# Seven products in the first feed-forward stage as in the other two; state-space parameters divided over the first two of these stages

## The chip, the cores and the metric

The kernel runs on one core of a Trainium2 chip. The core has five engines with a queue of instructions each: TensorE (PE in the profile; its weight loads are PEld), VectorE (DVE), ScalarE (ACT), GpSimd (POOL) and SyncE (SP, which issues the DMAs). Each queue is executed in order, and engines wait for each other by semaphores. The metric is device time of one execution in microseconds.

## The reference

A stack of three blocks on x of 512 positions by 1024 features, all in float32. The first two blocks (`hybrid_layer`, layers 0 and 1) mix by attention, a convolution and retention, and then feed forward with 4096 hidden features. The third (`second_block`) mixes by differential attention and a state-space layer and then feeds forward with a gated stage of 2816. Cut to what the change touches:

```
def hybrid_layer(x, ...):
    ...                                        # mixing, x = x + rms_norm(mix)
    h = rms_norm(x, g_mlp_pre)
    f = jnp.square(jax.nn.relu(h @ w_up)) @ w_down
    return x + rms_norm(f, g_mlp_post)

def s5_layer(u, a_re, a_im, log_dt, b_re, b_im, c_re, c_im, ...):
    dt = jnp.exp(log_dt)[:, None]
    mag = jnp.exp(a_re * dt)
    lb_re, lb_im = mag * jnp.cos(a_im * dt), mag * jnp.sin(a_im * dt)
    ...                                        # cr, ci; bb = (cr, ci) * b
    _, _, xr, xi = lax.associative_scan(...)   # a complex linear recurrence over positions
```

What the state-space layer needs of `dt`, `lb` and `b`, `c` depends on the weights alone, so it can be computed at any time before the third block.

## The kernel before

**Precision.** A float32 matmul is made of three passes over operands split into a high part (fp32r) and the rest: high by high, high by low, low by high (`mm3`). Every weight chunk (128x1024, 512 KB) is loaded into `wraw`, its high part is written by ScalarE or VectorE into `whi`, and the rest by VectorE or GpSimd into `wlo`. Which of the two is set by `wbias`: 3 leans to GpSimd, 1 keeps it on VectorE.

**A feed-forward stage.** The normalised input stands transposed in `hhi`/`hlo` (8 blocks of 128 features by 512 positions). A block of 128 hidden features is made (up), passed through square-ReLU into `fhi`/`flo`, and each group of four blocks is multiplied by its part of `w_down` into eight accumulators `acc` (down). The first four blocks are made in two halves of the positions (`f_split`), which overlaps with the end of the normalisation.

Two forms of up exist. In the plain form (`mlp_plain`, layer 0) a block is 8 x 3 matmuls of 512 columns. In the form with seven products (`mlp`, layer 1, and `ffn2` in the third block) two blocks are made together: weights and input are halved along features and positions, and seven products of sums of halves (4 x 3 matmuls of 256 columns each) give the four quarters that eight products gave. The sums and splits of the input are made once (`fast_in`, tiles `sraw`, `shi`, `slo`), those of the weights for each pair (`take_fast`, tiles `wsum`), and the quarters are put together while they leave the accumulators (`FastUp.out`, tiles `mid` and `cu`), all on VectorE and ScalarE. Four of the 32 blocks stay plain, so there are 14 pairs. In this form X is written to DRAM at the start of the stage (`spill`) and read back at its end. `FAST` (line 48) lists the layers that use it; it also sets the order of the weight stream.

**The parameters of the state-space layer** are a side task, a generator that adds its instructions in portions. `ssm_params` (line 1802) first computes on tiles of 128x32 (`prm`) on VectorE with three functions on ScalarE, then eight combinations of 128x512 on GpSimd (`sbc` is the input, results go to DRAM as `gd` and `hd`), then powers of a rotation (`pw`), then eight tables of sines and cosines: two memsets on VectorE, 42 doubling steps on GpSimd (tiles `t`), and at the end one multiply by a sign on VectorE,

```
V.tensor_scalar(Sn, Sn, sgn, None, op0=ALU.mult)
```

which must wait for GpSimd. `yield 3000` says that the next portion is due 3 us later.

**The order of the work** is made ahead of time by a planner (`Trace.order`). It goes through a planned run with a cost for each operation: of the operations whose inputs are ready, an engine takes the one that is due first, and only those due within 25.16 us of the matmul stream's position. The queues of the engines are fixed by it. What the plan takes for shorter or longer than it is shows on the chip as a wait in a queue.

Of the kernel before, what the change touches and what calls it, by code (L numbers as in the profile page):

```python
# [44 lines left out]


NF2 = DFF2 // 128
FAST = (1,)


def mlp_groups():
# [116 lines left out]
PV = {}  # L168
# [768 lines left out]
class Builder:  # L937
# [711 lines left out]
    def mlp_plain(self, l, X):  # L1649
        nc = self.nc  # L1650
        groups = mlp_groups()
        self.wbias = 3
        if l == 0:
            self.side.add(self.ssm_params(), 40000)
        acc = [None] * NT
        f = {}
        last_g = len(groups) - 1

        def relu2(m):
            def ev(ps):  # L1660
                r = self.s2()
                nc.vector.tensor_scalar(r, ps, 0.0, None, op0=ALU.max)
                hi, lo = self.s2(F32R, "fhi"), self.s2(F32R, "flo")
                nc.scalar.activation(hi, r, AF.Square)
                nc.scalar.activation(r, r, AF.Square)
                nc.vector.tensor_tensor(lo, r, hi.bitcast(F32), op=ALU.subtract)
                f[m] = (hi, lo)
            return ev
        lhs = lambda k, t0, t1: tuple(z[:, t0:t1] for z in f[k])
        for g, (k0, n) in enumerate(groups):  # L1670
            if g == 0:
                self.f_split([relu2(i) for i in range(n)], self.mid_start((1, 3)))
                gpost = self.load_gain(4 * l + 3)
                nxt = 4 * (l + 1) if l + 1 < LAYERS else 8
                gpre = self.load_gain(nxt)
            else:
                for i in range(n):
                    self.f_unit(relu2(k0 + i))
                self.down(groups[g - 1], lhs, acc, f, g == 1)
        xd = [[self.dp.tile(F32, f"xd{l}_{t}_{h}", [P, 512]) for h in range(2)] for t in range(NT)]  # L1680

        def store(t):
            for h in range(2):
                nc.sync.dma_start(out=xd[t][h], in_=X[t][h])
        self.finish_plain(groups[-1], lhs, acc, X, gpost, gpre, store)
        self.xd = xd
# [21 lines left out]
    def mlp(self, l, X):  # L1708
        nc = self.nc
        self.wbias = 1  # L1710
        self.seven = True
        xm = self.spill(X, f"xm{l}")
        del X
        f, acc = {}, [None] * NT
# [87 lines left out]
    def ssm_params(self):  # L1802
# [34 lines left out]
        mag = new()  # L1837
        nc.scalar.activation(mag, x, AF.Exp)
        ang = mul(aim, dt)
        yield 3000  # L1840
        k = x
        V.tensor_scalar(k, ang, 1.0 / (2 * math.pi), 12582912.0, op0=ALU.mult, op1=ALU.add)
        V.tensor_scalar(k, k, -12582912.0, None, op0=ALU.add)
# [5 lines left out]
            V.scalar_tensor_tensor(r, k, -c, r, op0=ALU.mult, op1=ALU.add)  # L1849
        V.tensor_scalar(r, r, -3.1415925, 3.1415925, op0=ALU.max, op1=ALU.min)  # L1850
        si, co = new(), new()
        yield 3000
        nc.scalar.activation(si, r, AF.Sin)
        V.scalar_tensor_tensor(co, r, -1.0, r, op0=ALU.mult, op1=ALU.max)
        V.tensor_scalar(co, co, -1.0, math.pi / 2, op0=ALU.mult, op1=ALU.add)
        nc.scalar.activation(co, co, AF.Sin)
        yield 3000
        lb = (mul(mag, co), mul(mag, si))
        nr = new()
        V.tensor_scalar(nr, lb[0], -1.0, None, op0=ALU.add)  # L1860
# [2 lines left out]
        mul(aim, aim, s1)  # L1863
        add(den, s1, den)
        V.reciprocal(den, den)
        yield 3000
        cr, ci = new(), new()
        mul(nr, are, s1)
        mul(lb[1], aim, s2_)
# [3 lines left out]
        mul(nr, aim, s2_)  # L1873
        sub(s1, s2_, s1)
        mul(s1, den, ci)
        yield 3000
        ms = k
        mul(mag, mag, ms)
        self.mag4 = mul(ms, ms)
# [26 lines left out]
        for t in range(4):  # L1906
            V.tensor_scalar(q, d[1], nsg[:, 0:1], None, op0=ALU.mult)
            combine(d[0], q, sb[0], sb[1], self.gd[3 - t])
            yield 3000
            if t < 3:  # L1910
                d = cmul(d, lb, d)
                yield 3000
        ee = (d[0], d[1])
        V.tensor_copy(ee[0], lb[0])
        V.tensor_copy(ee[1], lb[1])
# [1 line left out]
        for t in range(4):  # L1917
            V.tensor_scalar(q, ee[0], sgn, None, op0=ALU.mult)
            V.tensor_scalar(q2, ee[1], -1.0, None, op0=ALU.mult)
            combine(q, q2, sb[2], sb[3], self.hd[t])  # L1920
            yield 3000
            if t < 3:
                ee = cmul(ee, lb, ee)
                yield 3000
        del sb
        ph = cmul((co, si), (co, si))
        ph = cmul(ph, ph, ph)
# [1 line left out]
        for j in range(7):  # L1929
            if j:  # L1930
                ph = cmul(ph, ph)
            pw.append(ph)
            yield 3000
        self.ctd = [self.dp.tile(F32, f"ctd{i}", [P, 512]) for i in range(8)]
        self.std = [self.dp.tile(F32, f"std{i}", [P, 512]) for i in range(8)]
        for b in range(8):
# [4 lines left out]
            for j in range(7):  # L1941
# [9 lines left out]
                G.tensor_tensor(t_, c0, pi, op=ALU.mult)  # L1951
                G.tensor_tensor(s1_, s1_, t_, op=ALU.add)
                if j > 3:
                    yield 3000
            V.tensor_scalar(Sn, Sn, sgn, None, op0=ALU.mult)
            nc.sync.dma_start(out=self.ctd[b], in_=C)
            nc.sync.dma_start(out=self.std[b], in_=Sn)
            yield 3000


    def ssm_task(self, us, ud, yd):
# [394 lines left out]
```

## Time and profile before

| | us |
|---|---|
| time, median of 3 runs | 2094.49 (2093.89 to 2096.01) |
| the profiled execution, its own time | 2094.96 |
| its span, first to last instruction | 2093.2 |

| stretch of the span | us |
|---|---|
| first feed-forward stage, from its first evacuation to its first output normalisation | 282.8 to 618.5 |
| second feed-forward stage, the same | 900.5 to 1213.3 |
| third feed-forward stage | about 1750 to the end |

Line 674 is the helper that issues every operation, so the profile's groups are told apart by tiles, not by lines. A row of the timeline has start, duration, engine, operation, written tile and read tiles, and in brackets how long the engine stood before it and for whom.

### The profile page before, as it was taken

The page shows a single profiled execution, that of the slowest core. Times are in us where ns is not written, and L with a number is a line of the kernel's source. Part 1 is how long each engine was busy: PE and PEld are TensorE (multiplying, and loading weights), DVE is VectorE, ACT ScalarE, POOL GpSimd, SP SyncE. Part 2 cuts the span into 40 slices and gives each one's busy share as a digit, 9 for nine tenths or more (in the row PEclk, how much of TensorE's full clock was granted, in tenths as well). Part 3 has the DMA queues.
Part 4 walks back from the last instruction along what each step waited for, and adds up shares of the span by engine and source line. Part 5 has one row for each costly group of instructions (what it writes and reads, how often), then busy time and mean ns, then how long its engine had stood idle before and what let it go on. Part 6 is the DMA issues. An engine that isn't in the chain of part 4 may idle for free. (4 is left out here: it accounts for less than half of the span.)

```text
span 2093.2 us, 30000 instructions
## 1 busy us (share of the span) xinstructions
PE 2009.5 (96%) x11188; PEld 1741.6 (83%) x11188; DVE 1523.1 (73%) x2487; ACT 1041.7 (50%) x1773; POOL 689.2 (33%) x844
## 2 busy tenths in 40 slices
PE   7999999999999999999999999889999999999999
PEld 7988788877888987799988987678777889989998
DVE  5999578534457999576776773688589649889887
ACT  3378443222334387454443445367577336545543
POOL 4662325993104663100000037753663430000000
PEclk9999999999999999999999999999999999999999
DMA  5423234333232422223422564231325422333322
GB/s 191 134 61 121 89 116 133 126 107 111 86 121 91 134 89 103 101 81 94 128 90 92 181 208 118 83 92 55 116 66 169 158 81 61 101 101 101 121 81 91
DMA packets 87874, 229.53 MB, mean 110 GB/s; under 512 B 10673, under 2 KB 20657, under 8 KB 87729
## 3 DMA queue, kind: packets, MB, share of 16 engines
q1 hardware_dynamic: 87728, 227.62, 34.1%
q8 instruction: 88, 1.44, 0.3%
q14 instruction: 58, 0.47, 0.1%
HBM read 206.35 MB, written 21.23 MB: 109 GB/s over the span
## 5 line engine op out<-in xcount | busy, mean ns | idle before, releaser
L674 ACT CAST whi<-wraw 128x1024 fp32r<-128x1024 f32 (+1 forms) x324 | 331.6, 1030 | 439.2 <-PE ps L674 360.2
L674 POOL TENSOR_TENSOR wlo<-wraw,whi 128x1024 fp32r<-128x1024 f32 (+1 forms) x142 | 333.3, 2354 | 488.5 <-ACT whi L674 399.8
L674 PE MATMUL ps<-hhi,whi 128*128 128x256 f32 (+1 forms) x1488 | 453.5, 330 | 8.6 <-DVE acc L674 2.9
L674 PE MATMUL ps<-hlo,whi 128*128 128x256 f32 (+1 forms) x1488 | 451.4, 328 | 10.3 <-DVE hlo L674 10.3
L674 PE MATMUL ps<-hhi,wlo 128*128 128x256 f32 (+1 forms) x1488 | 449.7, 328 | 1.2 <-DVE wlo L674 1.2
L674 PEld LDWEIGHTS ps<-hlo,whi 128*128 128x128 f32 x1488 | 272.3, 193 | 34.7 <-DVE hlo L674 11.5
L674 PEld LDWEIGHTS ps<-hhi,whi 128*128 128x128 f32 x1488 | 272.3, 193 | 34.1 <-issue 3.3
L674 PEld LDWEIGHTS ps<-hhi,wlo 128*128 128x128 f32 x1488 | 271.4, 193 | 24.2 <-DVE wlo L674 1.4
L674 DVE TENSOR_TENSOR wlo<-wraw,whi 128x1024 fp32r<-128x1024 f32 x192 | 237.4, 1242 | 64.9 <-ACT whi L674 64.9
L674 PE MATMUL ps<-whi,fhi 128*128 128x512 f32 x688 | 251.3, 393 | 5.0 <-DVE acc L674 4.2
L674 PE MATMUL ps<-wlo,fhi 128*128 128x512 f32 x688 | 251.8, 392 | 1.6 <-DVE wlo L674 1.6
L674 PE MATMUL ps<-whi,flo 128*128 128x512 f32 x688 | 252.5, 392 | 0.0
L674 DVE TENSOR_TENSOR acc<-ps,acc 128x512 f32<-128x512 f32 x112 | 75.9, 686 | 116.5 <-PE ps L674 116.4
L674 PE MATMUL ps<-whi,hhi 128*128 128x384 f32 (+1 forms) x448 | 153.5, 367 | 5.2 <-DVE vlo L674 3.5
L674 PE MATMUL ps<-wlo,hhi 128*128 128x384 f32 (+1 forms) x448 | 153.9, 367 | 1.2 <-POOL wlo L674 1.2
L674 PEld LDWEIGHTS ps<-whi,fhi 128*128 128x128 f32 x688 | 129.4, 189 | 29.0 <-DVE acc L674 4.6
L674 PE MATMUL ps<-whi,hlo 128*128 128x384 f32 (+1 forms) x448 | 152.7, 367 | 0.0
L674 PEld LDWEIGHTS ps<-wlo,fhi 128*128 128x128 f32 x688 | 129.7, 189 | 26.7 <-DVE wlo L674 2.9
L674 PEld LDWEIGHTS ps<-whi,flo 128*128 128x128 f32 x688 | 129.7, 189 | 24.4
L674 PE MATMUL ps<-shi,whi 128*128 128x256 f32 (+1 forms) x440 | 124.3, 292 | 0.6 <-ACT mid L674 0.6
L674 PE MATMUL ps<-slo,whi 128*128 128x256 f32 (+1 forms) x440 | 124.2, 291 | 0.0
L674 PE MATMUL ps<-shi,wlo 128*128 128x256 f32 (+1 forms) x440 | 124.0, 290 | 0.0
(272 smaller groups left out, 3887.5 us busy)
## 6 DMA issues: line engine op xcount, KB each, us to landing
wraw<-in_wst SPq DMA_DIRECT2D x302, 512.0 KB, 3.7
wraw<-in_wst SPq DMA_DIRECT2D x32, 384.0 KB, 3.1
gain<-in_gains SPq DMA_DIRECT2D x20, 256.0 KB, 4.9
X<-in_x SPq DMA_DIRECT2D x16, 256.0 KB, 5.4
xd<-X SPq DMA_DIRECT2D x16, 256.0 KB, 2.4
X<-xd SPq DMA_DIRECT2D x16, 256.0 KB, 5.7
gated<-t SPq DMA_DIRECT2D x16, 256.0 KB, 2.2
gate<-gated SPq DMA_DIRECT2D x16, 256.0 KB, 4.2
```

Of the source, the lines that this page charges most:

```text
L674: getattr(getattr(self.nc, e), m)(*[r(x) for x in op.args], **{k: r(v) for k, v in op.kw.items()})
```

## The change

Layer 0 joins the form with seven products, so `mlp_plain` is no longer called, and its weights are split on VectorE alone (`wbias` 1 in place of 3). `ssm_params` is cut in two: what comes before the tables is added at the start of the first feed-forward stage, the tables (`ssm_tables`) at the start of the second. Both begin 30 us of planned time after the stage (40 before), and their portions are due every 7 and 8 us instead of every 3.

```
-FAST = (1,)
+FAST = (0, 1)
...
     def mlp_plain(self, l, X):
...
-        if l == 0:
-            self.side.add(self.ssm_params(), 40000)
...
     def mlp(self, l, X):
         nc = self.nc
         self.wbias = 1
         self.seven = True
+        self.side.add((self.ssm_params, self.ssm_tables)[l](), 30000)
         xm = self.spill(X, f"xm{l}")
...
     def ssm_params(self):
...
-        yield 3000
+        yield 7000
...
             pw.append(ph)
-            yield 3000
+            yield 7000
+        self.pw = pw
+
+    def ssm_tables(self):
+        nc, V, pw = self.nc, self.nc.vector, self.pw
+        o, w = PV["sgn"]
+        sgn = self.pvt[:, o:o + w]
         self.ctd = [self.dp.tile(F32, f"ctd{i}", [P, 512]) for i in range(8)]
         self.std = [self.dp.tile(F32, f"std{i}", [P, 512]) for i in range(8)]
         for b in range(8):
...
                 if j > 3:
-                    yield 3000
+                    yield 8000
             V.tensor_scalar(Sn, Sn, sgn, None, op0=ALU.mult)
             nc.sync.dma_start(out=self.ctd[b], in_=C)
             nc.sync.dma_start(out=self.std[b], in_=Sn)
-            yield 3000
+            yield 8000
```

All other `yield 3000` of `ssm_params` become `yield 7000`.

TensorE in the first feed-forward stage, up, before: blocks of 512 columns, here of two accumulators in turn.

```order
L674 MATMUL ps_3521<-hhi_355,whi_3327 128x512
L674 MATMUL ps_3455<-hhi_355,wlo_3300 128x512
L674 MATMUL ps_3521<-hlo_356,whi_3327 128x512
L674 MATMUL ps_3455<-hhi_355,whi_3285 128x512
L674 MATMUL ps_3521<-hhi_355,wlo_3344 128x512
L674 MATMUL ps_3455<-hlo_356,whi_3285 128x512
```

At the same place now: part of one of the seven products, with the sums `shi`/`slo` as its input.

```order
L674 MATMUL ps_3423<-shi_3484,whi_3413 128x256
L674 MATMUL ps_3423<-slo_3512,whi_3413 128x256
L674 MATMUL ps_3423<-shi_3484,wlo_3438 128x256
L674 MATMUL ps_3423<-shi_3495,whi_3413 128x256
L674 MATMUL ps_3423<-slo_3521,whi_3413 128x256
L674 MATMUL ps_3423<-shi_3495,wlo_3438 128x256
```

What moved: the same up products of 28 blocks are now 1176 matmuls of 256 columns instead of 672 of 512. Outside the first stage TensorE's order is the same but for three places of some ten instructions in the second.

VectorE in the first stage, beginning of the parameters, before: `t<-ps` are evacuations of up, `prm16` is the operand that GpSimd's combination reads, the rest of `prm` leads to it.

```order
L674 TENSOR_SCALAR t_3494<-sbc_3447,pv_412 128x512
L674 TENSOR_TENSOR prm1_3394<-prm13_3460,prm9_3413 128x32
L674 TENSOR_SCALAR t_3501<-ps_3392 128x512
L674 TENSOR_TENSOR wlo_3507<-wraw_3319,whi_3491 128x1024
L674 TENSOR_TENSOR prm13_3460<-prm2_3489,prm1_3394 128x32
L674 COPY prm12_3429<-prm0_3380 128x32
L674 TENSOR_SCALAR prm16_3469<-prm13_3460,prm15_3416 128x32
L674 TENSOR_TENSOR flo_3528<-t_3501,fhi_3509 128x512
L674 TENSOR_SCALAR t_3549<-ps_3455 128x512
```

The same portion now, the end of a run of 19 such instructions; `cu<-ps,mid` is an evacuation of a product.

```order
L674 TENSOR_TENSOR prm2_3736<-prm12_3728,prm10_3685 128x32
L674 TENSOR_TENSOR prm0_3632<-prm0_3632,prm1_3688 128x32
L674 TENSOR_TENSOR prm13_3742<-prm0_3632,prm3_3074 128x32
L674 TENSOR_SCALAR prm16_3745<-prm13_3742,prm15_3640 128x32
L674 TENSOR_TENSOR prm0_3632<-prm12_3728,prm9_3711 128x32
L674 TENSOR_TENSOR prm1_3688<-prm13_3742,prm10_3685 128x32
L674 TENSOR_TENSOR prm0_3632<-prm0_3632,prm1_3688 128x32
L674 TENSOR_TENSOR prm1_3688<-prm13_3742,prm9_3711 128x32
L674 COPY prm12_3728<-prm0_3632 128x32
L674 TENSOR_TENSOR prm13_3742<-prm2_3736,prm1_3688 128x32
L674 TENSOR_SCALAR prm16_3745<-prm13_3742,prm15_3640 128x32
L674 TENSOR_TENSOR cu_3822<-ps_3770,mid_3762 128x256
```

What moved: before, evacuations and splits stood between the parameters' instructions; now the first two writes of `prm16` come with nothing between them but such instructions, ahead of an evacuation.

VectorE at the tables, before, in the first stage: memsets of one table (`t_4853`, `t_4855`), then the sign multiply of the table before it (`t_4659`).

```order
L674 MEMSET t_4853 128x4
L674 MEMSET t_4855 128x4
L674 TENSOR_TENSOR flo_4860<-t_4827,fhi_4839 128x512
L674 TENSOR_SCALAR t_4889<-ps_4790 128x512
L674 TENSOR_TENSOR wlo_4897<-wraw_4777,whi_4884 128x1024
L674 TENSOR_TENSOR flo_4914<-t_4889,fhi_4900 128x512
L674 TENSOR_SCALAR t_4932<-ps_4851 128x512
L674 TENSOR_TENSOR wlo_4942<-wraw_4798,whi_4924 128x1024
L674 TENSOR_SCALAR t_4659<-t_4659,pv_412 128x512
L674 TENSOR_TENSOR flo_4962<-t_4932,fhi_4940 128x512
L674 TENSOR_TENSOR acc_3629<-ps_4926,acc_3629 128x512
```

Now, in the second stage: the sign multiply of a table (`t_9992`), and after it the memsets of the next.

```order
L674 TENSOR_SCALAR cu_10232<-cu_10232 128x512
L674 TENSOR_TENSOR wlo_10328<-wraw_10236,whi_10307 128x1024
L674 TENSOR_SCALAR t_9992<-t_9992,pv_412 128x512
L674 TENSOR_TENSOR wlo_10351<-wraw_10259,whi_10332 128x1024
L674 TENSOR_TENSOR flo_10363<-cu_10232,fhi_10342 128x512
L674 TENSOR_TENSOR cu_10370<-ps_10224,mid_10360 128x256
L674 TENSOR_TENSOR wsum_10375<-wraw_10278,wraw_10313 128x512
L674 MEMSET t_10382 128x4
L674 MEMSET t_10384 128x4
```

What moved: tables no longer overlap, and between a table's memsets and its sign multiply stand 70, 21, 18, 24, 38, 37, 22 and 35 VectorE instructions (9 to 18 before).

## Rows read from the trace of the kernel before

**Rows 1.** The page: the span, and busy time by engine.

```profile
span 2093.2 us, 30000 instructions
...
PE 2009.5 (96%) x11188; PEld 1741.6 (83%) x11188; DVE 1523.1 (73%) x2487; ACT 1041.7 (50%) x1773; POOL 689.2 (33%) x844
```

**Rows 2.** Timeline of VectorE at the bounds of two stages: start us, duration us.

```profile
282.82 0.69 DVE L674 TENSOR_SCALAR t<-ps 128x512 f32<-128x512 f32 x1 [4.08 <-PE ps L674]
...
618.52 1.41 DVE L674 SCALAR_TENSOR_TENSOR t<-acc,st,gain 128x512 f32<-128x512 f32 x2 [0.66 <-POOL st L674]
...
900.54 0.69 DVE L674 TENSOR_SCALAR cu<-ps 128x512 f32<-128x512 f32 x1 [0.25 <-PE ps L674]
...
1213.33 1.41 DVE L674 SCALAR_TENSOR_TENSOR t<-acc,st,gain 128x512 f32<-128x512 f32 x2 [0.66 <-POOL st L674]
```

**Rows 3.** Stretches: length, PE PEld DVE ACT POOL busy (count), clock, DMA, GB/s.

```profile
244.40:282.80 38.40, 32.73 (x207) 29.57 (x207) 27.63 (x41) 15.89 (x35) 10.40 (x9) 0.91 0.31 96
282.80:618.50 335.70, 327.82 (x1461) 271.50 (x1461) 186.24 (x334) 108.77 (x141) 166.10 (x367) 0.98 0.37 118
618.50:660.00 41.50, 37.56 (x245) 34.31 (x244) 31.24 (x45) 18.19 (x42) 14.15 (x12) 0.96 0.29 99
864.90:900.50 35.60, 32.59 (x208) 29.45 (x207) 31.47 (x52) 22.31 (x55) 4.70 (x7) 0.95 0.33 116
900.50:1213.30 312.80, 312.80 (x1966) 283.48 (x1965) 216.64 (x320) 146.64 (x226) 3.63 (x4) 1.00 0.36 113
1213.30:1255.00 41.70, 36.52 (x237) 33.12 (x236) 34.11 (x56) 21.30 (x48) 13.68 (x11) 0.92 0.74 235
313.00:365.00 52.00, 52.00 (x231) 43.07 (x230) 43.26 (x123) 20.09 (x27) 29.04 (x35) 1.00 0.43 137
423.00:434.00 11.00, 6.81 (x20) 5.06 (x19) 1.80 (x5) 0.00 (x0) 10.77 (x44) 0.69 0.13 50
434.00:500.00 66.00, 62.31 (x267) 50.77 (x266) 32.20 (x42) 21.77 (x27) 54.42 (x133) 0.97 0.38 126
1960.00:2060.00 100.00, 97.80 (x702) 91.58 (x701) 89.17 (x131) 57.26 (x90) 0.00 (x0) 1.00 0.33 111
```

**Rows 4.** Timeline of TensorE: matmuls of 512 and of 256 columns.

```profile
412.23 0.39 PE L674 MATMUL ps<-wlo,fhi 128*128 128x512 f32 x1
...
423.11 0.39 PE L674 MATMUL ps<-whi,flo 128*128 128x512 f32 x1
427.69 0.80 PE L674 MATMUL ps<-whi,fhi 128*128 128x512 f32 x1 [4.19 <-DVE acc L674]
...
428.71 0.63 PE L674 MATMUL ps<-hhi,wlo 128*128 128x512 f32 x1
...
432.12 0.63 PE L674 MATMUL ps<-hlo,whi 128*128 128x512 f32 x1
...
896.14 0.28 PE L674 MATMUL ps<-hlo,whi 128*128 128x256 f32 x1
...
897.10 0.28 PE L674 MATMUL ps<-hhi,whi 128*128 128x256 f32 x1
```

**Rows 5.** Timeline of VectorE: two of the eight sign multiplies.

```profile
426.52 0.49 DVE L674 TENSOR_SCALAR t<-t,pv 128x512 f32<-128x512 f32 x1 [9.77 <-POOL t L674]
...
487.90 2.60 DVE L674 TENSOR_SCALAR t<-t,pv 128x512 f32<-128x512 f32 x1 [4.61 <-POOL t L674]
```

**Rows 6.** Waits from 290 to 660 us: total us, times, longest us.

```profile
DVE t L674 <- POOL t L674: 48.1, 8, 9.8
```

**Rows 7.** Timeline of GpSimd: the start of the first table.

```profile
361.74 0.51 POOL L674 TENSOR_TENSOR t<-t,prm 128x4 f32<-128x4 f32 x3 [16.62 <-DVE t L674]
```

**Rows 8.** Stretch 282 to 500 us, instructions on `prm` alone: DVE, ACT, POOL.

```profile
282.00:500.00 218.00, 34.70 (x140) 0.90 (x4) 100.21 (x240) 0.98 0.39 127
```

**Rows 9.** Groups on VectorE, 313 to 500 us, then 900.5 to 1213.3.

```profile
L674 DVE TENSOR_TENSOR wlo<-wraw,whi 128x1024 fp32r<-128x1024 f32 x29 | 37.9, 1309 | 2.5 <-ACT whi L674 2.5
...
L674 DVE TENSOR_TENSOR wlo<-wraw,whi 128x1024 fp32r<-128x1024 f32 x59 | 71.6, 1222 | 12.0 <-ACT whi L674 12.0
```

More of the change, by code (lines that the diff above doesn't have):

```diff
@@ L47 @@
 NF2 = DFF2 // 128
-FAST = (1,)
+FAST = (0, 1)
 def mlp_groups():
@@ L1652, in mlp_plain @@
         self.wbias = 3
-        if l == 0:
-            self.side.add(self.ssm_params(), 40000)
         acc = [None] * NT
@@ L1711, in mlp @@
         self.seven = True
+        self.side.add((self.ssm_params, self.ssm_tables)[l](), 30000)
         xm = self.spill(X, f"xm{l}")
@@ L1839, in ssm_params @@
         ang = mul(aim, dt)
-        yield 3000
+        yield 7000
         k = x
@@ L1851, in ssm_params @@
         si, co = new(), new()
-        yield 3000
+        yield 7000
         nc.scalar.activation(si, r, AF.Sin)
@@ L1856, in ssm_params @@
         nc.scalar.activation(co, co, AF.Sin)
-        yield 3000
+        yield 7000
         lb = (mul(mag, co), mul(mag, si))
@@ L1865, in ssm_params @@
         V.reciprocal(den, den)
-        yield 3000
+        yield 7000
         cr, ci = new(), new()
@@ L1875, in ssm_params @@
         mul(s1, den, ci)
-        yield 3000
+        yield 7000
         ms = k
@@ L1908, in ssm_params @@
             combine(d[0], q, sb[0], sb[1], self.gd[3 - t])
-            yield 3000
+            yield 7000
             if t < 3:
                 d = cmul(d, lb, d)
-                yield 3000
+                yield 7000
         ee = (d[0], d[1])
@@ L1920, in ssm_params @@
             combine(q, q2, sb[2], sb[3], self.hd[t])
-            yield 3000
+            yield 7000
             if t < 3:
                 ee = cmul(ee, lb, ee)
-                yield 3000
+                yield 7000
         del sb
@@ L1932, in ssm_params, with ssm_tables @@
             pw.append(ph)
-            yield 3000
+            yield 7000
+        self.pw = pw
+    def ssm_tables(self):
+        nc, V, pw = self.nc, self.nc.vector, self.pw
+        o, w = PV["sgn"]
+        sgn = self.pvt[:, o:o + w]
         self.ctd = [self.dp.tile(F32, f"ctd{i}", [P, 512]) for i in range(8)]
@@ L1953, in ssm_params @@
                 if j > 3:
-                    yield 3000
+                    yield 8000
             V.tensor_scalar(Sn, Sn, sgn, None, op0=ALU.mult)
@@ L1957, in ssm_params @@
             nc.sync.dma_start(out=self.std[b], in_=Sn)
-            yield 3000
+            yield 8000
     def ssm_task(self, us, ud, yd):
```

## The prediction

> **What bounds the kernel now.** I read the page first. TensorE is busy for 2009.5 of 2093.2 us, 96%, while VectorE has 73%, ScalarE 50% and GpSimd 33% [rows 1]. So a change pays if it takes matmul time away or closes one of TensorE's gaps; what it does to the other engines counts only where TensorE comes to wait for them. The profiled execution took 2094.96 us, 1.8 us more than its span, and stands 0.5 us above the median of the runs shown (2094.49). The sum below is made against 2094.96.
>
> The second view is VectorE's timeline, for landmarks. The body of a feed-forward stage runs from the first square-ReLU evacuation (282.82 and 900.54) to the first normalisation of the finished output (618.52 and 1213.33) [rows 2]. It lasts 335.7 us in the first stage and 312.8 us in the second. Both stages have the same sizes; the first is written plainly, the second with seven products. The second stage is therefore a measured model of what the first one becomes, and 22.9 us is the first figure to explain.
>
> The third view, busy time by stretch, says where the 22.9 us lie. The second body has TensorE busy for all 312.80 us at clock 1.00, the first for 327.82 of 335.70 at 0.98 [rows 3]. The reader is to see that the plain stage is not only longer in work: it has holes.
>
> **Products.** Fourteen pairs of feature blocks change form. A pair needed 2 x 8 x 3 = 48 matmuls of 512 columns and needs 7 x 4 x 3 = 84 of 256. At full clock 48 steps from 412.23 to 423.11 give 0.2267 us for one of 512, and 8 steps from 896.14 to 897.10 give 0.120 us for one of 256 [rows 4]. A pair goes from 10.88 to 10.08 us; 14 pairs save 11.2 us. An eighth of the columns is saved, but a short matmul pays relatively more around it, so only 7.4% of the time is.
>
> The Trainium skill ("TensorE: Matmul & The Clock Gate", section "Back-to-back issue gap") gives an isolated gap of N/2.4 + 2.5 ns, which is 215.8 and 109.2 ns here. By it, as an estimate, the pairs would save 14 x (10.36 - 9.17) = 16.6 us and the time would be 5.4 us lower. The trace does not agree: it has 226.7 and 120 ns, and the sum goes by the trace.
>
> **The holes.** 22.9 - 11.2 leaves 11.7 us. From 423 to 434 us TensorE ran 20 matmuls in 11.0 us, which need 4.5 at full clock: 6.5 us lost. From 434 to 500, 267 matmuls need 60.5 of 66.0 us: 5.5 us lost [rows 3]. Together 12.0, so these two stretches are the whole remainder. The cause is on view: TensorE stands for 4.19 us for an accumulation on VectorE, and then runs at half clock (8 steps of 0.426 us from 428.71 to 432.12) [rows 4]. VectorE was late because it stood 9.77 us until 426.52 for a GpSimd tile, the sign multiply at the end of a table [rows 5]. In the first stage it did so 8 times, 48.1 us in all [rows 6]. The first table's work began at 361.74 on GpSimd and the last sign multiply is at 487.90 [rows 7, 5]: eight tables in 126.2 us, 15.8 us each, on a GpSimd that also took weight splits and was busy for 10.77 of 11 us in the worst stretch [rows 3].
>
> The change takes the tables out of the first stage, so both stalls leave it. What is late there next is VectorE's own load (below). I take the body at the second stage's 312.8 us: **-22.9 us**.
>
> **The parameters stay in the first stage.** They are 140 small VectorE instructions, 34.7 us [rows 8], which the model stage lacks. 216.6 + 34.7 = 251.3 us is 80% of 312.8. They are spread over 26 pauses of 7 us, 182 us of planned time; there VectorE has 69% + 19% = 88%. The nearest rows: with the same instructions and VectorE at 83% (43.26 of 52) TensorE lost nothing; at 89%, in the third stage, it lost 2.2 us of 100 [rows 3]. So 0 to 4.0 us. 88% is nearer to the second row, but these instructions are short and leave gaps between them: I take **+3.0**. Their densest place is a run of 19 between a weight split and a product's evacuation, with two writes of one operand that GpSimd must have read in between. Behind it in VectorE's queue stands that evacuation, and behind that TensorE. GpSimd has only these combinations there, since all weight splits of the stage move to VectorE and are in the 216.6 already.
>
> **The stage's two ends.** Entry, 38.4 us before, is 35.6 us in the model with 207 against 208 matmuls: between -2.8 and 0; I take **-2.0**, as that is the nearer model. Exit: TensorE's unused time is 5.2 us in the model's 41.7 and 3.9 in the first stage's 41.5 [rows 3]: between 0 and +1.2; the matmul order there hardly changes, I take **+0.5**. The 8 spills and 8 reloads of X at 256 KB each lie beside matmuls, with the DMA engines 36 to 37% busy in both bodies [rows 3]; if that cover were gone they would show as entry or exit, which the bounds hold.
>
> **The tables in the second stage.** VectorE gets eight sign multiplies at 0.49 us [rows 5] and 16 tiny memsets: 216.6 + 3.9 is 71% of the body. The wait is what matters. Before, the order starts the next table while one is unfinished; now a table's memsets come only after the last one's sign multiply, with 18 to 70 VectorE instructions in between. This body runs 320 instructions in 312.8 us, 0.98 each [rows 3], so the shortest distance is 17.6 us against 15.8 us of GpSimd work, and GpSimd has no weight splits there (3.63 us busy). Behind a waiting sign multiply stand a weight split and an evacuation. Bounds: 0, and 11.7 if all stalls move along; every row of the order speaks for the low end, I take **+0.5**.
>
> Of GpSimd beside VectorE the rows show this: a weight split on VectorE took 1309 ns on average while GpSimd was busy, against 1222 ns where it was idle [rows 9], 7% more. The Trainium skill ("SBUF — State Buffer", section "Who interferes with whom") says more: of a VectorE instruction with two SBUF inputs and a GpSimd one that reads SBUF, the second to issue fully blocks. That rule speaks against this change; as a mechanism it is rival 3, and the 7% bear it out only in part.
>
> **Sum.** -22.9 + 3.0 - 2.0 + 0.5 + 0.5 = -20.9 us: 2094.96 - 20.9 = 2074 us. The order of the mixing stages and of the third stage does not change on TensorE, so nothing is counted there. With every bound at its end the likeliest case reaches from 2069 (-22.9 - 2.8) to 2079 (-22.9 + 4.0 + 1.2 + about 1.5 for two short waits in the second stage).
>
> **Rivals.**
> 1. VectorE overfills in the parameters' stretch. For: 88% on average, and the run of 19. Against: 83% did no harm. Each late evacuation costs a stop like the one at 423 us, 6.5 us with its half clock; two stops in place of the 3.0 give 2084. Chance 0.13.
> 2. The sign multiplies still wait. For: 17.6 against 15.8 us is close at one table. Against: the other seven have more room, GpSimd is otherwise idle. With both old stalls back, 11.7 us: 2086 (the 0.5 included there). Chance 0.07.
> 3. Slower: GpSimd's table work blocks VectorE in the second stage instruction by instruction. The tables took at most 126.2 us of GpSimd. If all of it held VectorE, 220.5 + 126.2 = 346.7 us of VectorE work would stand in a body of 312.8, 33.9 us longer: 2108. It decides from the point where more than 92 us are blocked. Against: +7% on the splits, some 15 us on 216.6. Chance 0.03.
> 4. The change does not shorten the products: splits and sums for the seven products arrive too late in the first stage and TensorE waits for what it saved, 11.2 us: 2085. Against: the second stage does the same with no gap. Chance 0.04.
>
> **From this to the numbers.** Forecast 0.73, rivals 0.13, 0.07, 0.03, 0.04. A measurement of this kernel tells about 0.2%, 4.2 us, from no change: below 2090.3 is faster. Only rival 3, or rivals 1 and 2 together with more than two stops, get past that: faster 0.94, within 0.2% 0.03, slower 0.03. The range of 8 in 10 takes the forecast's 2069 to 2079, two more below for an entry that gains more than the model, and rival 1: 2067 to 2084.
>
> **What would show it.** The first body at 313 to 317 us with TensorE at clock 1.00 and no gap over a microsecond behind an accumulation. VectorE waiting for GpSimd tiles for less than 8 us in the two stages together. Matmuls of 256 columns at 0.120 us in the first stage. The second body within 1 us of 312.8. Wrong would be: holes of several microseconds in the first third of the first body (rival 1), sign multiplies with waits of 5 us or more in the second (rival 2), splits on VectorE over 1.5 us there (rival 3).

## The result, and the profile after

The changed kernel took 2076.68 us, median of 4 runs (2075.80 to 2077.58), against 2095.25 us for the kernel before in the same set: a ratio of 0.9914 (95% interval 0.9902 to 0.9925), 18.6 us faster. Forecast were 2074 us and a range of 2067 to 2084. The profiled execution took 2077.58 us. The four runs fall into two pairs: 2077.5 us at a mean granted clock of 0.991, and 2075.8 at 0.993.

The page first: the span, and busy time by engine. TensorE's busy time fell by 9 us against [rows 1], VectorE's rose by 72. Most of that is the sums of weight and input blocks and their splits, which the seven products need. Of the plain weight splits only seven moved: VectorE makes 199 of them instead of 192, since `wbias` 3 had left GpSimd no more than 8 in the first stage.

```profile
span 2075.9 us, 31293 instructions
...
PE 2000.3 (96%) x11692; PEld 1757.3 (85%) x11692; DVE 1594.8 (77%) x2636; ACT 1085.6 (52%) x1881; POOL 689.2 (33%) x837
```

Then VectorE's timeline at the marks of [rows 2]: the first evacuation and the first normalisation of the output, in both stages.

```profile
280.22 0.69 DVE L674 TENSOR_SCALAR cu<-ps 128x512 f32<-128x512 f32 x1 [0.23 <-PE ps L674]
...
592.96 1.42 DVE L674 SCALAR_TENSOR_TENSOR t<-acc,st,gain 128x512 f32<-128x512 f32 x2 [0.66 <-POOL st L674]
...
880.27 0.68 DVE L674 TENSOR_SCALAR cu<-ps 128x512 f32<-128x512 f32 x1
...
1195.70 1.41 DVE L674 SCALAR_TENSOR_TENSOR t<-acc,st,gain 128x512 f32<-128x512 f32 x2 [0.67 <-POOL st L674]
```

The first body lasts 312.7 us (before 335.7), the second 315.4 (before 312.8). The stretches, with the columns of [rows 3], say what TensorE did in them, and in the exit of the first stage:

```profile
280.22:592.96 312.74, 312.74 (x1965) 283.55 (x1964) 238.97 (x447) 146.79 (x227) 35.27 (x26) 1.00 0.38 126
880.27:1195.70 315.43, 313.21 (x1946) 282.84 (x1945) 224.82 (x343) 145.42 (x225) 124.48 (x298) 0.99 0.38 125
...
592.90:634.50 41.60, 37.30 (x223) 33.62 (x222) 31.10 (x45) 17.31 (x40) 13.25 (x12) 0.88 0.29 98
```

The first body has no hole left: TensorE busy all the time, at full clock, with the parameters beside it. The second body, which had none before, has two now, of 0.48 us at 890 and 1.74 us at 1021, and the exit's clock fell from 0.96 to 0.88. The waits of VectorE for table tiles, 48.1 us before [rows 6], are nearly gone:

```profile
DVE t L674 <- POOL t L674: 2.6, 2, 2.3
```

TensorE's two longest stops in the exit, and the longer one of the second body with matmuls behind it:

```profile
607.59 0.66 PE L674 MATMUL ps<-cm,t 128*128 128x128 f32 x4 [1.66 <-DVE t L674]
...
610.36 1.11 PE L674 MATMUL ps<-cm,t 128*128 128x128 f32 x4 [1.88 <-DVE t L674]
...
1021.26 0.39 PE L674 MATMUL ps<-shi,whi 128*128 128x256 f32 x1 [1.74 <-DVE cu L674]
...
1022.89 0.41 PE L674 MATMUL ps<-hhi,whi 128*128 128x256 f32 x1
...
1025.24 0.42 PE L674 MATMUL ps<-hhi,wlo 128*128 128x256 f32 x1
```

The stop at 1021 costs more than its 1.74 us in this execution: the 11 steps from 1022.89 to 1025.24 are 0.214 us each, not 0.120. In the second profiled execution of the same kernel ("changed, again" below) the same stop, 1.72 us, is there, but the clock stays up behind it. From 1021 to 1026 us, here and there (26 and 36 matmuls, clock 0.66 and 1.00):

```profile
1021.00:1026.00 5.00, 4.74 (x26) 4.70 (x27) 2.60 (x5) 2.06 (x6) 0.00 (x0) 0.66 0.81 249
...
1021.00:1026.00 5.00, 4.84 (x36) 4.67 (x37) 3.66 (x8) 3.42 (x7) 0.00 (x0) 1.00 0.74 231
```

The lower clock is worth 1.7 us, about the difference between the two executions in the second stage (353.7 and 352.2 us). No sign multiply is near the stop. VectorE in front of it, and GpSimd beside it:

```profile
1010.26 0.95 DVE L674 TENSOR_TENSOR wsum<-wraw 128x512 f32<-128x512 f32 x1
...
1016.07 1.76 DVE L674 TENSOR_TENSOR wlo<-wraw,whi 128x1024 fp32r<-128x1024 f32 x1
...
1018.77 0.96 DVE L674 TENSOR_SCALAR cu<-cu 128x512 f32<-128x512 f32 x1
...
1020.79 0.74 DVE L674 TENSOR_TENSOR cu<-ps,mid 128x256 f32<-128x256 f32 x2
```

```profile
1015.03 1.72 POOL L674 TENSOR_TENSOR t<-t 128x256 f32<-128x256 f32 x1
1016.82 1.48 POOL L674 TENSOR_TENSOR t<-t,prm 128x256 f32<-128x256 f32 x1
1018.38 1.06 POOL L674 TENSOR_TENSOR t<-t 128x256 f32<-128x256 f32 x1
```

Each of the first three VectorE rows lies on a table step and is longer than its kind (the sum of 512 takes 0.68 us elsewhere, the split 1.22, the in-place step 0.42), and the evacuations at the end come late.

### The profile page after: what moved, and what is told of

Its sections match the earlier page's. It is cut to its first block, busy times and chain, and to the rows that moved or that the text cites. A ratio compares the mean times of both kernels' runs of the same rounds, so it can differ in the third digit from the quotient of the medians.

```text
span 2075.9 us, 31293 instructions
## 1 busy us (share of the span) xinstructions
PE 2000.3 (96%) x11692; PEld 1757.3 (85%) x11692; DVE 1594.8 (77%) x2636; ACT 1085.6 (52%) x1881; POOL 689.2 (33%) x837
## 5 line engine op out<-in xcount | busy, mean ns | idle before, releaser
L674 POOL TENSOR_TENSOR wlo<-wraw,whi 128x1024 fp32r<-128x1024 f32 (+1 forms) x135 | 311.5, 2313 | 552.1 <-ACT whi L674 499.4
L674 PE MATMUL ps<-hhi,whi 128*128 128x256 f32 (+1 forms) x1488 | 426.8, 314 | 4.5 <-ACT hhi L674 2.0
L674 PE MATMUL ps<-hlo,whi 128*128 128x256 f32 (+1 forms) x1488 | 424.5, 312 | 6.6 <-DVE hlo L674 6.6
L674 PE MATMUL ps<-hhi,wlo 128*128 128x256 f32 (+1 forms) x1488 | 422.9, 312 | 1.2 <-DVE wlo L674 1.2
L674 DVE TENSOR_TENSOR wlo<-wraw,whi 128x1024 fp32r<-128x1024 f32 x199 | 245.0, 1239 | 64.8 <-ACT whi L674 64.6
L674 PE MATMUL ps<-shi,whi 128*128 128x256 f32 (+1 forms) x608 | 169.7, 291 | 2.8 <-DVE cu L674 1.7
L674 ACT COPY mid<-ps 128x256 f32<-128x256 f32 x144 | 52.9, 368 | 228.2 <-PE ps L674 228.0
L674 PE MATMUL ps<-slo,whi 128*128 128x256 f32 (+1 forms) x608 | 169.1, 289 | 0.0
L674 PE MATMUL ps<-shi,wlo 128*128 128x256 f32 (+1 forms) x608 | 168.7, 289 | 0.0
```

The source lines that it names most:

```text
L674: getattr(getattr(self.nc, e), m)(*[r(x) for x in op.args], **{k: r(v) for k, v in op.kw.items()})
```

## The experiments

One table for all. "First" is the first feed-forward stage, from the first normalisation in its entry (`t<-ps,st,gain`, 244.38 us before) to its first output normalisation; "between" is its exit and the mixing stage; "second" is the second feed-forward stage, bounded like the first. All three are from VectorE's timeline of one profiled execution, and differ by up to 0.4% between executions of one kernel (353.7 and 352.2 us below); times are medians, ratios go against the kernel before in the same set.

| kernel | time | ratio (95%) | first | between | second |
|---|---|---|---|---|---|
| before | 2095.3 | | 374.1 | 246.4 | 348.4 |
| changed | 2076.7 | 0.9914 (0.9902–0.9925) | 348.4 | 249.1 | 353.7 |
| changed, again | 2077.8 | 0.9913 (0.9900–0.9927) | 348.4 | 249.0 | 352.2 |
| division alone | 2086.6 | 0.9957 (0.9945–0.9970) | 362.2 | 246.4 | 353.7 |
| products alone | 2113.7 | 1.0092 (1.0076–1.0107) | 388.1 | 249.0 | 348.5 |
| no table steps | 2074.1 | 0.9900 (0.9887–0.9914) | 349.2 | 249.0 | 348.4 |
| parameters doubled | 2076.0 | 0.9910 (0.9897–0.9924) | 347.0 | 249.1 | 352.0 |
| tables later | 2075.9 | 0.9908 (0.9894–0.9921) | 348.4 | 248.4 | 350.6 |
| exit on VectorE | 2074.1 | 0.9900 (0.9887–0.9914) | 346.7 | 249.0 | 352.6 |
| short pauses | 2109.7 | 1.0071 (1.0057–1.0084) | 357.1 | 248.1 | 377.1 |
| one stage, spaced | 2093.4 | 0.9990 (0.9981–0.9999) | 369.9 | 248.1 | 348.4 |
| later, and exit | 2075.8 | 0.9905 (0.9891–0.9918) | 347.8 | 249.1 | 350.9 |
| short, no combinations | 2074.5 | 0.9901 (0.9887–0.9914) | 348.5 | 247.5 | 352.4 |
| tables on VectorE | 2073.0 | 0.9891 (0.9875–0.9908) | 348.4 | 248.2 | 348.5 |

**Division alone.** The first stage stays plain; parameters go into it and tables into the second, with the new pauses.

```
-FAST = (0, 1)
+FAST = (1,)                # and in mlp_plain, l == 0: side.add(self.ssm_params(), 30000)
```

> The first stage stays plain; only the parameters and tables are divided over the first two stages, with the spacing of 7 and 8 us. Theory (the gain has two parts that add up, 11.2 us of products and 11.7 us of stalls behind table tiles, and the second stage gives about 4 us back where GpSimd's table steps hold up VectorE): first body 335.7 - 11.7 = 324 us, no sign multiplies and no stop of 4 us in it; entry and body of the second stage 3 to 4 us longer than before; time 2094.96 - 11.7 + 4 = 2087, between 2084 and 2090. Rival A (the whole gain is the products', the stalls only changed place): time 2093 to 2098. Rival B (nothing is lost in the second stage for the tables, what the changed kernel lost there comes with the earlier start): time 2083 or less, second body 312.8.

Measured 2086.6. The first stage became 11.9 us shorter, and TensorE has no hole in it (the stretch begins 1.05 us before the first evacuation; by the marks of [rows 2] the body is 322.9 us):

```profile
282.50:606.40 323.90, 323.90 (x1470) 269.84 (x1469) 170.50 (x300) 109.17 (x139) 51.10 (x33) 1.00 0.36 110
```

The second stage is 5.3 us longer, as in the changed kernel, with the same stop of 1.74 us. So the loss there comes with the tables and not with an earlier start. The run changes two things, the place of the tasks and their pauses.

**Products alone.** Seven products in the first stage, parameters and tables whole in it, pauses of 3 us.

```
-FAST = (1,)
+FAST = (0, 1)
...
+        if l == 0:
+            self.side.add(self.ssm_params(), 40000)     # in mlp; yields of 3000
```

> The first stage has seven products; parameters and tables stay whole in it, with pauses of 3 us. Theory (two parts that add up): 11.2 us for the products, the table stalls stay at least in part, since sign multiplies still wait in VectorE's queue; second stage as before, 312.8. Time 2094.96 - 11.2 - 2 for the entry = 2082, between 2078 and 2086, and VectorE waits for GpSimd tiles in the first stage for over 15 us. Rival A (the whole gain is the products', dividing brings nothing): 2077 or below, as the changed kernel. Rival C (products without the division are worth nothing, since VectorE, now with the weight splits, and the tables collide): 2090 or more, with several stops of 4 us or more in the first body.

Measured 2113.7: 19 us slower than before. The theory of two parts that add up falls; rival C had it. VectorE stood as long for table tiles as before (45.8 us in 7 waits, against 48.1 in 8), but the first stage went from 374.1 to 388.1 us. One of these waits, and the stop that it makes:

```profile
427.65 0.56 DVE L674 TENSOR_SCALAR t<-t,pv 128x512 f32<-128x512 f32 x1 [9.48 <-POOL t L674]
...
428.74 0.41 DVE L674 TENSOR_TENSOR cu<-ps,mid 128x256 f32<-128x256 f32 x1
```

```profile
429.20 0.58 PE L674 MATMUL ps<-shi,whi 128*128 128x256 f32 x1 [6.41 <-DVE cu L674]
```

Behind the sign multiply in VectorE's queue stands the evacuation of a product, and TensorE gets it 1.6 us after the wait ends. Five stops of 3.1 to 6.4 us come to 23.5 us here; in the plain stage there were three of 0.8 to 4.2, 7.9 us together. Four of the five, 18.5 us, follow the wait of a sign multiply: such a wait costs more in the form with seven products. The fifth, 4.98 us at 378.38, follows no wait. In front of it VectorE is busy for 12.09 of 12.40 us, most of it with 54 steps of the parameters in front of an evacuation, the later ones near their own length (instructions on `prm` alone; DVE, ACT, POOL):

```profile
365.90:378.30 12.40, 9.09 (x54) 0.00 (x0) 6.80 (x21) 0.89 0.18 69
```
Why this form has less work in front of TensorE (VectorE's work with all splits on it, 257.8 us in this body against 186.2 [rows 3], or the accumulators that a pair holds) was not separated.

**Short pauses.** The changed kernel with 3 us in place of 7 and 8; stages divided as changed.

```
-            yield 7000      # tables: 8000
+            yield 3000
```

> The changed kernel with pauses of 3 us, as before, in place of 7 and 8; parameters in the first stage and tables in the second as in the changed kernel. Theory (the pauses decide: with 3 us the order starts a table while GpSimd still has the last one, and VectorE stands for it with a seven-product evacuation behind it, as in the run with the products alone): VectorE waits over 25 us for table tiles in the second stage, stops of 4 us or more there, second body 20 to 40 us longer, time 2095 to 2117. Rival G (the division decides, parameters and tables in one stage are too much for VectorE together): waits under 8 us, 2075 to 2080.

Measured 2109.7. VectorE waits 34.5 us for table tiles, and the second stage is 28.7 us longer than before, with stops of 9.83, 8.42 and 3.70 us. So the division alone does not protect: the pauses decide, as the theory had it. But the two longest of these stops came by another queue than VectorE's. SyncE issues the DMAs in order, and there the store of a table (`ctd<-t`) waited for GpSimd, with four weight loads behind it; ScalarE then stood for the first of these weights longer than VectorE did for its sign multiply:

```profile
933.20 0.33 SPq L674 DMA_DIRECT2D wraw<-in_wst  x1
947.22 0.32 SPq L674 DMA_DIRECT2D ctd<-t  x1
947.63 1.83 SPq L674 DMA_DIRECT2D wraw<-in_wst  x4
```

```profile
951.75 1.04 ACT L674 CAST whi<-wraw 128x1024 fp32r<-128x1024 f32 x1 [10.44 <-DMA wraw<-in_wst]
```

At the stop of 8.42 us ScalarE stood 9.72 us in the same way. No run separates the two queues. What the theory had not foreseen is the first stage, 357.1 and not 348.4 us, with no table in it:

```profile
329.55 0.58 PE L674 MATMUL ps<-shi,whi 128*128 128x256 f32 x1 [6.35 <-DVE cu L674]
```

VectorE before this stop, and GpSimd beside it:

```profile
316.05 2.65 DVE L674 TENSOR_TENSOR prm<-prm,prm 128x32 f32<-128x32 f32 x5
...
322.77 1.02 DVE L674 TENSOR_SCALAR prm<-prm,prm 128x32 f32<-128x32 f32 x1 [0.96 <-POOL t L674]
323.82 1.19 DVE L674 COPY prm<-prm 128x32 f32<-128x32 f32 x1
325.05 0.98 DVE L674 TENSOR_SCALAR prm<-prm 128x32 f32<-128x32 f32 x1
325.94 0.18 DVE L674 TENSOR_TENSOR prm<-prm,prm 128x32 f32<-128x32 f32 x1
...
329.07 0.42 DVE L674 TENSOR_TENSOR cu<-ps,mid 128x256 f32<-128x256 f32 x1
```

```profile
323.71 1.26 POOL L674 TENSOR_TENSOR t<-t 128x512 f32<-128x512 f32 x1
324.93 2.23 POOL L674 TENSOR_TENSOR t<-sbc,prm 128x512 f32<-128x512 f32 x2
```

A copy of 32 columns, 0.17 us elsewhere, took 1.19 us: it began 0.11 us after a GpSimd instruction and ended with it. VectorE stood for GpSimd only once here, 0.96 us; nearly all the rest is instructions that lasted longer.

**Short, no combinations.** The same pauses for the parameters, without the 24 GpSimd combinations; tables with 8 us.

```
-            nc.gpsimd.tensor_tensor(v3(o), v3(b), bc(a), op=ALU.mult)
-            ...
-            nc.sync.dma_start(out=dst, in_=o)
+            nc.sync.dma_start(out=dst, in_=b)
```

> The changed kernel with the parameters' pauses at 3 us (as in the run with dense pauses in both stages, whose first body had a stop of 6.35 us at 329.55 and took 322.8) but without the 24 GpSimd instructions that combine parameters with coefficients; the coefficients are stored as they are. So this leaves out a part of the computation. The tables keep their pauses of 8. Theory (GpSimd's combinations hold up the short parameter steps on VectorE, 0.18 us each, to a microsecond and more, and so the evacuation queued behind them): no stop over 2 us in the first body, 312.7 to 315 us, time 2075 to 2079. Rival H (so many parameter steps ahead of an evacuation are too much for VectorE by themselves): a stop of 4 us or more near 330 stays, first body 318 to 323, time 2081 to 2087.

Measured 2074.5, the first stage 348.5, no stop in its body. VectorE in the same place:

```profile
314.78 0.74 DVE L674 TENSOR_TENSOR prm<-prm,prm 128x32 f32<-128x32 f32 x4
...
319.56 0.74 DVE L674 TENSOR_TENSOR prm<-prm,prm 128x32 f32<-128x32 f32 x5
```

Five steps take 0.74 us and not 2.65. From 310 to 340 us VectorE runs 87 instructions here in 25.9 us busy; beside the combinations it ran 51 in 28.6. So contention with GpSimd makes this stop, not the number of steps. (The stop at 378 in the run with the products alone shows that enough steps in one run can make one as well.)

**Parameters doubled.** The changed kernel; each two-operand step of the parameters is issued twice.

```
+            V.tensor_tensor(dup, a, b, op=op)
             V.tensor_tensor(o, a, b, op=op)
```

> The changed kernel with each two-operand step of the parameters issued twice on VectorE (first into a spare tile), some 100 more instructions of 0.19 us, 19 us more of VectorE work in the first body, most of it from 312 to 480 us. Theory (VectorE's load does not set the price, TensorE has enough finished work in front of it as long as VectorE stays under 100% over some 20 us): first body 312.7 to 314, time 2077 to 2079. Rival E (the price rises with the load, as the prediction had it, 3 us at 88%): VectorE at about 90% there, 3 us or more lost, time 2080 to 2084, with stops behind accumulations.

Measured 2076.0, as the theory had it. Stretch 312 to 480 us:

```profile
312.00:480.00 168.00, 168.00 (x1059) 152.22 (x1058) 153.16 (x389) 77.67 (x119) 30.06 (x24) 1.00 0.35 116
```

VectorE is busy for 91% (changed kernel: 136.9 us, 82%) and TensorE loses nothing. The average load of VectorE is not the price.

**No table steps.** The changed kernel without the doubling steps; two memsets fill each table.

```
-                G.tensor_tensor(c1_, c0, pr, op=ALU.mult)      # and five more
-            V.memset(Cv[:, :, 0:1], 1.0)
+            V.memset(C, 1.0)
```

> The changed kernel without the 336 doubling steps of the tables on GpSimd; each table is filled by two memsets on VectorE instead, sign multiplies and stores stay. So this leaves out a part of the computation. Theory (in the second stage GpSimd's table steps stretch VectorE's instructions with two inputs from SBUF): second entry and body back at 35.6 and 312.8 us, wsum at 0.68 and wlo at 1.22 us throughout, no stop at 1021; 4.3 us gained on the changed kernel, 2073, between 2072 and 2074.5. Rival D (the 3 to 4 us come from the order, the sign multiplies and stores that stay in VectorE's and SP's queues): 2076.5 to 2078.5, with the stop still there.

Measured 2074.1, at the upper edge of the theory's 2072 to 2074.5. The second stage is back at 348.4, 5.3 us shorter; its entry takes 35.9 us, against 38.3 in the changed kernel and 35.6 before. VectorE in the place of the stop at 1021:

```profile
1008.84 0.69 DVE L674 TENSOR_TENSOR wsum<-wraw 128x512 f32<-128x512 f32 x1
...
1013.31 1.22 DVE L674 TENSOR_TENSOR wlo<-wraw,whi 128x1024 fp32r<-128x1024 f32 x1
...
1015.05 0.42 DVE L674 TENSOR_SCALAR cu<-cu 128x512 f32<-128x512 f32 x1
```

The same order, each row at its own length, and no stop: rival D falls. Of the 5.3 us only 2.6 show in the median; the rest of the program was some 2 us longer in this profile, and why is open.

**Tables later**: 60 us after the stage's start and not 30.

```
-        self.side.add((self.ssm_params, self.ssm_tables)[l](), 30000)
+        self.side.add((self.ssm_params, self.ssm_tables)[l](), (30000, 60000)[l])
```

> The changed kernel with the tables planned 60 us after the start of the second stage and not 30. TensorE's and ScalarE's orders are the same as in the changed kernel. Theory (GpSimd's table steps stretch VectorE's two-input instructions wherever they meet a dense stretch of them): no table step before the body, so the second entry is back at about 35.7 to 36 us and TensorE gains 1 us there; the fourth table meets another stretch, so the stop of 1.74 us at 1021 goes or moves; time between 2073.5 (both gone) and 2077 (a stop elsewhere). Rival D (order and stores): entry and stop stay as they are, 2076.7, the stop still at 1021.

Measured 2075.9 (2072.7 to 2077.8): its gain can't be told from none. The trace is clear, though: the entry is back (35.6 us, from 38.3), the stop at 1021 is gone, and smaller ones stand at 975 and 980, where table steps meet a dense stretch:

```profile
975.36 0.39 PE L674 MATMUL ps<-shi,whi 128*128 128x256 f32 x1 [0.31 <-DVE cu L674]
979.98 0.39 PE L674 MATMUL ps<-hhi,whi 128*128 128x256 f32 x1 [0.55 <-ACT mid L674]
```

**Exit on VectorE.** The second mixing stage's first weight splits, which run in the first stage's exit, stay on VectorE.

```
-        self.wbias = 2
+        self.wbias = 1 if l else 2      # 2 again after the stage's first unit
```

> The changed kernel with the first weight splits of the second mixing stage kept on VectorE; from the stage's first unit on they may go to GpSimd again. They run in the exit of the first feed-forward stage. Theory (there a split on GpSimd held the normalisation on VectorE for 5.66 us where two such instructions take 1.4): the pair takes about 1.4 us, the stops of 1.66 and 1.88 us shrink, exit and mixing together come from 249.0 back to 246.4 and the time to 2073.5 to 2075. Rival F (VectorE has the exit's longest queue, and the splits added to it, 1.2 us each, cost what is gained; the 2.7 us belong to the seven products' exit itself): 2076 to 2080.

In the changed kernel the exit had, on VectorE and on GpSimd:

```profile
604.65 5.66 DVE L674 SCALAR_TENSOR_TENSOR t<-X,st,gain 128x512 f32<-128x512 f32 x2
```

```profile
604.62 5.14 POOL L674 TENSOR_TENSOR wlo<-wraw,whi 128x1024 fp32r<-128x1024 f32 x2 [0.45 <-ACT whi L674]
```

With the splits on VectorE, this pair is short, but another is held beside the one split that GpSimd still makes (608.65 to 610.45), and TensorE has one long stop for three short ones:

```profile
603.33 0.74 DVE L674 SCALAR_TENSOR_TENSOR t<-X,st,gain 128x512 f32<-128x512 f32 x1
...
608.65 3.01 DVE L674 SCALAR_TENSOR_TENSOR t<-acc,st,gain 128x512 f32<-128x512 f32 x2 [0.44 <-POOL st L674]
```

```profile
613.52 0.58 PE L674 MATMUL ps<-hlo,whi 128*128 128x256 f32 x1 [5.50 <-DVE hlo L674]
```

"Between" stays at 249.0: the theory was right on the instruction and wrong on the time. In the changed kernel it is 2.7 us longer than before (in all kernels with seven products 1.1 to 2.8; with division alone it is not), and the rows say where most of that is: in TensorE's clock. In the changed exit TensorE stands idle for 4.3 us against 3.9 before, but its clock of 0.88 over 41.6 us is 5.0 us lost, against 1.7 us at 0.96 [rows 3]. With the splits on VectorE the clock is 0.92 over the same stretch, 3.3 us lost, and TensorE stands idle for 6.3: what one gave, the other took. Why the lower clock lasts longer behind these stops stays open. The median is 2.6 us lower than the changed kernel's, but the intervals of the two ratios overlap, and most of what the profile shows gained lies in the first stage, where nothing was expected.

**One stage, spaced.** Parameters and tables both in the first stage.

```
-        self.side.add((self.ssm_params, self.ssm_tables)[l](), 30000)
+        if l == 0:
+            self.side.add(self.ssm_params(), 20000)     # yields of 2500
+            self.side.add(self.ssm_tables(), 90000)     # yields of 6000
```

> Seven products in the first stage with parameters and tables both in it, but the tables spaced: parameters from 20 us on with pauses of 2.5 us, tables from 90 us on with pauses of 6. Theory (the pauses decide): sign multiplies wait under 10 us in all, first body 313 to 320 us, second entry and body back at 35.7 and 312.8, so 2073 to 2081. Rival G (the division decides): waits and stops as in the run with the products alone, 2090 or more.

Measured 2093.4, outside the theory's range. The second stage is clean, 348.4; the first has stops of 5.63 us at 329.8 (in the parameters, as with short pauses) and 7.19 at 395.9, and VectorE waits 11.5 us for table tiles. The stop at 395.9 came by SyncE's queue again: weight loads stood behind a table's store until 389, and ScalarE stood 8.4 us for them. One stage does not give both tasks the room; as both pauses are shorter than in the changed kernel, the run does not settle whether the place matters by itself.

**Later, and exit.** The two edits together, beside the changed kernel again.

> The two edits of the runs before together: tables 60 us after the start of the second stage, and the first weight splits of the second mixing stage kept on VectorE. It is tried as a version that could beat the changed kernel. Theory (each gap is a meeting of GpSimd with a dense stretch of VectorE, and moving one makes the next): second entry at 35.7 us, one small stop left in the second body, the exit as long as before in sum; 2072 to 2075 against 2076 to 2077.5 for the changed kernel in the same set, 2 to 4 us. Rival (the two bring nothing that a measurement can tell): within 2 us of the changed kernel.

> The changed kernel unaltered, for comparison within this set: 2076 to 2077.5 us, with the stop of 1.74 us near 1021 by every theory.

2075.8 against 2077.8, 1.9 us: less than the 2 to 4 us of the theory, as the rival had it, and below what the intervals of the ratios tell apart. The stop at 1021 stood again in the unaltered kernel (1.72 us).

**Tables on VectorE.** Tables later, with the doubling steps on VectorE.

```
-                G = nc.gpsimd
+                G = nc.vector
```

> The run with the tables 60 us after the start of the second stage, with the 336 doubling steps on VectorE and not on GpSimd. It is tried as a version that could beat the changed kernel. Theory (what costs is GpSimd beside VectorE, not VectorE's load): VectorE gets some 336 steps of 0.07 to 0.4 us, 40 to 60 us more, up to about 88% of the second body, and still TensorE loses under 1 us there: second entry 35.7, body 312.6 to 314, no instruction of VectorE stretched, time 2072 to 2075. Rival E (VectorE's load sets the price): stops behind evacuations in the second body, 2077 to 2085.

Measured 2073.0 (2071.4 to 2075.0), the best of all: ratio 0.9891. The second body:

```profile
876.85:1189.69 312.84, 312.84 (x1965) 283.48 (x1964) 275.28 (x680) 146.61 (x226) 4.63 (x4) 1.00 0.39 126
```

VectorE is busy for 88%, and TensorE has no gap. A weight split takes 1220 ns on average there, 1257 in the changed kernel. Against the changed kernel the ratio is some 0.2% lower; their intervals just overlap, while all 4 of its runs lie below all 9 of that kernel's, in other sets.

## Why the prediction held, and where its terms were off

By the three spans of the table, 25.7 us were gained in the first stage, 2.7 lost between, 5.3 lost in the second and 0.5 before the first and after the second: the profiled spans differ by 17.3 us. The forecast had 21.9 gained, 0.5, 0.5 and nothing. So 3.8 us more were gained in the first stage and 7.0 us more lost behind it: that the sum came within 3 us is in part luck, since the errors cancel.

- **The holes** (11.7 us): division alone takes 11.9 us from the first stage. Right, with the cause named: the sign multiplies' waits went from 48.1 to 2.6 us (2.3 with division alone).
- **Products, parameters, entry** (11.2 - 3.0 + 2.0 = 10.2 us): the step from division alone to the changed kernel takes 13.8 us from the first stage. The entry shrank by 2.8 us (38.44 to 35.66), at its bound. The body equals the model's 312.8, so the parameters cost nothing. **The step that failed is the parameters' price by VectorE's load**: an estimated 88% was held against a stretch of 89% in which 2.2 us were lost. VectorE was busy for 82% from 312 to 480 us and TensorE lost nothing; doubling the steps, at 91%, lost nothing either. What costs is late work in front of an evacuation at one place: steps that GpSimd held up (6.35 us with pauses of 3, the stop of rival 1 but for that other reason), or 54 steps within 12 us (4.98 us with the products alone). With pauses of 7 us GpSimd holds up single steps too, the longest at 350.20 for 1.33 us, but TensorE stops behind none.
- **The second stage** (0.5 us): 5.3 us in the profile, 3.8 in the second one of the same kernel. About half of it, 2.6 us, is in the stage's entry (38.3 against 35.6 us), for which the sum had no term, though the first table begins there, at 856 us. By TensorE, 2.3 us are stops; 1.7 us, in the first of the two profiles alone, are the lower clock; where the rest is, 1.3 to 1.5 us, was not found. The order kept the sign multiplies from waiting, as worked out; rival 2 did not come. Mis-sized was the contention that the prediction put into rival 3 and priced, at its upper end, as a block of everything. Its mechanism was there, at a small size: the second stage is back with the steps gone or on VectorE. The 126.2 us that it took as the most of GpSimd's work was too low: the steps took 118.3 us of GpSimd before and 140.8 here.
- **Exit** (0.5 us): "between" is 2.7 us longer, beyond the bound of 1.2. The bound was taken from TensorE's idle time, and that rose by 0.4 us, as forecast; the clock, which the term put at nothing, costs 3.3 us more. VectorE's normalisation held by weight splits on GpSimd is in the trace; removing it gained nothing.

The Trainium skill ("SBUF — State Buffer", section "Who interferes with whom") says that a VectorE instruction with two inputs from SBUF, or a copy in a mode with two ports, and a GpSimd instruction that reads SBUF exclude each other, and that the second to issue fully blocks. The prediction saw it borne out "only in part", by a mean of 7%. The single rows agree with it (the copy of 0.17 us that ended with the GpSimd instruction, 1.19 us later); in which mode that copy ran no trace here shows. That most splits met no GpSimd instruction is not the reason why their mean rose so little: of the 29 of [rows 9] 21 did. More often it was GpSimd that stood. In the changed kernel's second body 57 of its 298 instructions were over 0.1 us longer than the shortest of their kind, against 16 on VectorE. A table step there on 4 columns, 0.2 us elsewhere, and the weight split beside it:

```profile
1111.74 1.21 POOL L674 TENSOR_TENSOR t<-t 128x4 f32<-128x4 f32 x1
```

```profile
1111.66 1.23 DVE L674 TENSOR_TENSOR wlo<-wraw,whi 128x1024 fp32r<-128x1024 f32 x1 [0.50 <-ACT whi L674]
```

VectorE's instructions that read one of their operands from an accumulator were not held: 29 of these 50 lay on a GpSimd instruction, and the longest took 0.69 us.

```profile
L674 DVE TENSOR_TENSOR acc<-ps,acc 128x512 f32<-128x512 f32 x50 | 34.1, 686 | 48.3 <-PE ps L674 48.3
```

The sum was right for this change, but its terms are no prices of its parts. By the medians of each set, division alone gave 7.9 us, products alone cost 19.2, both together gave 18.6. The 11.2 us of the products are to be had only where no long wait, and no long run of small work, stands in VectorE's queue.

## What to carry to other kernels

Before work is spread in the pauses of a busy engine, look at what runs beside it: a VectorE at 88 to 91% cost nothing here, one at 71% was late where GpSimd ran beside it. Look, too, for every queue in which a result is waited for: here the store of a table held up weight loads in SyncE's queue, as its sign multiply held up evacuations in VectorE's. Read contention from single rows that are longer than their kind, not from a group's mean. Read TensorE's clock beside its idle time: a stage can lose more by a lower clock than by the stops before it. And of a change with two parts, one alone may lose where both together win, so test them apart before the sum is believed.

## What was not expected of the hardware

For their length, short instructions suffer most: on VectorE 128x32 steps of 0.17 to 0.19 us took up to 1.33 us beside GpSimd instructions of 1.1 to 1.3 us, while a split of 1.22 us rose to 1.76 at worst in the changed kernel; on GpSimd the step of 0.2 us above took 1.21. And one-input instructions were held as well: the copy above, a scalar operation of 0.98 us behind it, and the in-place step of 0.96 for 0.42. The doubling steps of the eight tables took 118.3 us of GpSimd before and 140.8 in the changed kernel, and on VectorE about 60: 275.3 against 216.6 us in the second body [rows 3], with the sign multiplies in it.
